# Two expert outputs per token: added in memory, or written side by side and added on chip

## The chip, the cores and the metric

The kernel runs on one core of a Trainium2 chip. The metric is the device time of one execution in microseconds (us). A core has a matrix engine (PE, with weight loads listed as PEld), a vector engine (DVE), a scalar engine (ACT), GpSimd (POOL) and a queue engine (SP) that issues most of the DMAs. GpSimd issues the DMAs whose rows are picked by a list of indices.

## The reference, cut to what matters

A transformer block runs first, then a hybrid layer on the same 1,024 tokens of width 1,024. The hybrid layer ends with a mixture of experts. Each token goes to two of 32 experts, so 2,048 token rows are spread over 32 lists, 64 rows to a list on average. Each expert is a gated pair of 1024x256 matrices and one 256x1024 matrix.

```python
def hierarchical_moe(h, ...):
    ...                                  # top group, then top-2 experts in it
    def expert_block(args):
        tok, wgt, e = args
        xb = h[tok]
        hid = jax.nn.silu(xb @ exp_gate[e]) * (xb @ exp_up[e])
        return (hid @ exp_down[e]) * wgt[:, None]
    ys = lax.map(expert_block, ...)
    return jnp.zeros((n, d), h.dtype).at[row_tok].add(ys.reshape(m_pad, d))

h = layer_norm_2(DEEPNORM_ALPHA * x + mixed, ln1_g, ln1_b)
ffn = hierarchical_moe(h.reshape(b * s, d), ...)
return layer_norm_2(DEEPNORM_ALPHA * h + ffn, ln2_g, ln2_b)
```

The output is the last norm of h plus the sum of the token's two expert rows. The kernel drops the common factor of h by scaling the weights and the epsilon.

## The kernel before, in words

All times and line numbers below are those of the profile. Until about 2,280 us the kernel runs the first block and the mixer. `output_mix` then makes h, 128 tokens at a time, and writes every piece to two scratch tensors in memory: `hd`, from which the experts read, and `acc`, to which they add (L1462). `route` builds, for each expert, a list of up to 128 token numbers and weights in `slots`; `tokens_of` turns it into integer row numbers `ids` (L1639). A place in a list that has no token points at one of 128 spare rows behind the last token.

`experts` runs a loop, written out in full, over 32 experts in a software pipeline. For expert e it gathers its 128 list places from `hd` (L1708; spare places are skipped by a bounds check), turns them with PE (L1719), splits rows and weights into a high and a low part (ACT L1695 and L1720, DVE L1696 and L1721), multiplies (L1731 to L1733), gates (L1738 to L1740), turns the hidden rows (L1747) and multiplies by the last matrix (L1762 to L1764). ACT scales the result into the tile `y` (L1765, two halves of 512 columns). There are three `y` buffers. Then GpSimd issues an indirect DMA that adds all 128 rows of `y` onto rows of `acc` (L1766):

```python
nc.gpsimd.indirect_dma_start(out=K.acc, out_offset=bass.IndirectOffsetOnAxis(ap=tok, axis=0), in_=y, in_offset=None,
                             compute_op=ALU.add)
```

The weights of an expert are three loads of 1 MiB from SP into a ring of ten `mraw` buffers (nine in one pool, one in another; L1663). In the texts here a *scatter* is the DMA of L1766, y(e) and scatter(e) are those of expert e, counted from 0.

After the loop SP loads the gain and bias of the last norm; `overflow` counts lists with more than 128 tokens and runs a loop over them whose number of turns is read from memory (none here). All engines pass that loop together. Behind it the last norm begins. SP loads eight tiles of `acc` (L1827, 128 tokens each, 0.5 MiB). Tiles 0, 2, 4 and 6 have their statistics made by DVE (L1842 to L1844), tiles 1, 3, 5 and 7 by ACT (L1836 to L1838) with a last multiply and bias by PE (L1856, L1857) and a copy by ACT (L1858). DVE multiplies by the gain in both (L1854, L1860) and finishes the even tiles (L1861). SP stores each tile (L1862).

The order on each engine is made at build time by a scheduler from the order of the program text. It puts a semaphore wait in front of an instruction that touches what an earlier one wrote; for a tensor in memory that is written through an index list it can't know which rows are meant.

Of the kernel before, what the change touches and what calls it, by code (L numbers as in the profile page):

```python
# [16 lines left out]
P = 128  # L17
# [1384 lines left out]
def output_mix(K, a, x2d, mixd, last, vs, aident, m, gains):  # L1402
# [5 lines left out]
    with ExitStack() as s:  # L1408
# [20 lines left out]
        for n_, tt in enumerate((4, 0, 1, 2, 3, 5, 6, 7)):  # L1429
            tsl = slice(tt * P, (tt + 1) * P)  # L1430
            v = vs[tt]
            at = slice(tt % 4 * P, (tt % 4 + 1) * P)
            mh, ml = (x[:, at] for x in last[tt // 4])
            stats = pool.tile([P, 2, 6], F, tag="lns", name=K.uid("lns"), bufs=2)
            if tt < KT // 2:
                src = v
                for c in range(2):
                    sl = slice(c * HB, (c + 1) * HB)
                    ps = pj.tile([P, HB], F, tag="pj", name=K.uid("pj"))
                    K.mm3(ps, mh, ml, wh[KT - 1][:, sl], wl[KT - 1][:, sl], True, True)  # L1440
                    nc.vector.tensor_tensor(v[c], ps, v[c], op=ALU.add)
                    nc.vector.bn_stats(stats[:, c], v[c])
            else:
                src = [None, None]

                def use(c, ps):
                    nc.vector.bn_stats(stats[:, c], ps)
                    src[c] = ps
                output_part(K, pj, "pj", x2d, mixd, aident, tt, v, use, [(mh, ml)])
            ex.ahead(n_)  # L1450
            mean, scale, shift = normalize(K, pool, stats, tt < KT // 2)
            for c in range(2):
                sl = slice(c * HB, (c + 1) * HB)
                if tt < KT // 2:
                    nc.scalar.activation(v[c], v[c], AF.Identity, bias=shift, scale=scale)
                    nc.vector.tensor_tensor(v[c], v[c], gain[c], op=ALU.mult)
                    nc.vector.tensor_tensor(v[c], v[c], bias[c], op=ALU.add)
                else:
                    nc.vector.scalar_tensor_tensor(v[c], src[c], mean, gain[c], op0=ALU.subtract, op1=ALU.mult)
                    nc.vector.scalar_tensor_tensor(v[c], v[c], scale, bias[c], op0=ALU.mult, op1=ALU.add)  # L1460
                for d in (K.hd, K.acc):
                    nc.sync.dma_start(d[tsl, sl], v[c])  # L1462
            pl = sm.tile([P, HB], F, tag="sm", name=K.uid("rl"))
            hts = []
            for g in range(2):
                pt = ht.tile([P, 4, P], F, tag="ht", name=K.uid("ht"))
                for q in range(4):
                    nc.tensor.transpose(pt[:, q], v[g][:, q * P:(q + 1) * P], K.ident)
                h_ = pool.tile([P, 4, P], F, tag=f"h{g}", name=K.uid("hT"), bufs=1)
                nc.scalar.activation(h_, pt, AF.Copy)  # L1470
                hts += [h_[:, q] for q in range(4)]
            for q in range(KT):
                nc.tensor.matmul(pl[:, :36], hts[q], wr[:, q], start=(q == 0), stop=(q == KT - 1))
            nc.vector.tensor_tensor(K.logits[:, tt], pl[:, :36], rb, op=ALU.add)
            if tt in (3, 5):
                places = route(K, pool, sm, *{3: (0, 4), 5: (4, 6)}[tt], "sm", dict(room=("room", 1), rows=("rows", 1), onehot=("onehot", 2)))
                places()
# [15 lines left out]
def routing_setup(K, pool):  # L1493
# [1 line left out]
    nc = K.nc  # L1495
    c = K.late
    K.hd = K.dram.tile([T + P, D], F, name="hd")
    K.acc = K.dram.tile([T + P, D], F, name="acc")
    K.logits = c.tile([P, KT, 36], F, name="logits")

    K.assign = c.tile([P, 4 + KT + 1, 32], R, name="assign")
# [10 lines left out]
    nc.gpsimd.iota(K.iota, pattern=[[1, P]], base=0, channel_multiplier=0, allow_small_or_imprecise_dtypes=True)  # L1512

    K.spare = c.tile([P, 1], F, name="spare")
    nc.gpsimd.iota(K.spare, pattern=[[0, 1]], base=T + 1, channel_multiplier=1, allow_small_or_imprecise_dtypes=True)
    K.slots = c.tile([P, 32, 2], F, name="slots")
    K.sent = c.tile([P, KT, 2, 3], F, name="sent")
    fill = pool.tile([P, HB], F, tag="NT", name="fill")
    nc.vector.memset(fill, 0.0)
    for c in range(2):  # L1520
        for d in (K.hd, K.acc):
            nc.sync.dma_start(d[T:T + P, c * HB:(c + 1) * HB], fill)


def route(K, pool, psum, t0, t1, tag, tags):
# [106 lines left out]
def tokens_of(K, pool, rows, n):  # L1632

    nc = K.nc
    m = pool.tile([P, n], F, name=K.uid("empty"))
    nc.vector.tensor_scalar(m, rows, 0.0, K.spare, op0=ALU.is_equal, op1=ALU.mult)
    nc.vector.scalar_tensor_tensor(m, rows, -1.0, m, op0=ALU.add, op1=ALU.add)
    ids = pool.tile([P, n], I32, name=K.uid("ids"))
    K.listed = nc.vector.tensor_copy(ids, m).ins  # L1639
    return ids  # L1640


class Experts:
# [29 lines left out]
def experts(K, a, ex, out):  # L1673
    nc, tc = K.nc, K.tc
    with ExitStack() as s:
# [75 lines left out]
            nc.vector.tensor_tensor(hl, pt[:, 0:2], hh.bitcast(F), op=ALU.subtract)  # L1751
            return hh, hl

        def down(hid, unit, tok, wgt):
            hh, hl = hid
            h, l = unit
            y = pool.tile([P, D], F, tag="y", name=K.uid("y"), bufs=3)
            for f in range(2):
                ps = yp.tile([P, HB], F, tag="y", name=K.uid("yps"))
                for q in range(2):  # L1760
                    sl = slice(q * D + f * HB, q * D + (f + 1) * HB)
                    nc.tensor.matmul(ps, hh[:, q], h[:, sl], start=q == 0, stop=False)  # L1762
                    nc.tensor.matmul(ps, hl[:, q], h[:, sl], start=False, stop=False)
                    nc.tensor.matmul(ps, hh[:, q], l[:, sl], start=False, stop=q == 1)  # L1764
                nc.scalar.activation(y[:, f * HB:(f + 1) * HB], ps, AF.Copy, scale=wgt)  # L1765
            nc.gpsimd.indirect_dma_start(out=K.acc, out_offset=bass.IndirectOffsetOnAxis(ap=tok, axis=0), in_=y, in_offset=None,  # L1766
                                         compute_op=ALU.add)

        def block(tok, wgt, eg, eu, ed):
            raws = [ex.load(w) for w in (eg, eu, ed)]  # L1770
            xg = gather(tok)
            units = [parts_of(raws, u) for u in range(3)]
            ps = gate_up(turned_rows(xg), units)
            down(turned_hidden(gated(ps)), units[2], tok, wgt)

        tok = lambda e: ids[:, e:e + 1]
        wgt = lambda e: K.slots[:, e, 1:2]
        raws = lambda e: [ex.raw[3 * e + i] for i in range(3)]
        NE = 32
        ex.ahead(ex.RAW + ex.MORE)  # L1780
        places = route(K, pool, tp, 6, KT, "tp", dict(room=("y", 3), rows=("sg", 2), onehot=("hh", 2)))
        ids = tokens_of(K, cst, K.slots[:, :, 0], 32)
        with tc.issue_after(K.listed):
            units = {0: [parts_of(raws(0), u) for u in range(3)]}
            places()
# [3 lines left out]
        for e in range(NE + 1):  # L1789
# [11 lines left out]
            if e < NE:  # L1801
                sg = gated(ps)
            if e > 0:
                down(hid.pop(e - 1), units.pop(e - 1)[2], tok(e - 1), wgt(e - 1))
            if n < NE:
                with tc.issue_after(K.listed) if e == 0 else nullcontext():
                    units[n].append(parts_of(raws(n), 1))
# [9 lines left out]
        g2, b2 = gains  # L1817

        nc.scalar.activation(pool.tile([P, 1], F, tag="sg", name="root"), K.ones[:, 0:1], AF.Sqrt)
        overflow(K, a, cst, tp, block, *ex.w)  # L1820

        v = [ex.pool.tile([P, 2048], F, tag="raw", name=K.uid("v"))[:, :D] for _ in range(KT - 1)]
        v.append(xgs[0])
        m = cst.tile([P, KT, 4], F, name="ln2m")
        stats = cst.tile([P, KT, 2, 6], F, name="ln2s")
        for tt in range(KT):
            nc.sync.dma_start(v[tt], K.acc[tt * P:(tt + 1) * P, :])  # L1827

        by_act = (1, 3, 5, 7)
        diag = [cst.tile([P, P], F, name=f"diag{i}") for i in range(2)]  # L1830
        for n0, n1 in ((0, 1), (1, 2), (2, 4), (4, 6), (6, 8)):
            for tt in range(n0, n1):
                if tt in by_act:
                    low = m[:, tt, 3:4]
                    junk = pool.tile([P, D], F, tag="y", name=K.uid("junk"), bufs=3)
# [3 lines left out]
                    nc.vector.tensor_scalar(m[:, tt, 2:3], m[:, tt, 1:2], 1.0 / D, EPS2, op0=ALU.mult, op1=ALU.add)  # L1839
                else:  # L1840
                    for c in range(2):
                        nc.vector.bn_stats(stats[:, tt, c], v[tt][:, c * HB:(c + 1) * HB])  # L1842
                    nc.vector.bn_aggr(m[:, tt, 0:2], stats[:, tt])
                    nc.vector.tensor_scalar(m[:, tt, 2:3], m[:, tt, 1:2], EPS2, None, op0=ALU.add)  # L1844
            r_ = sqrt_rsqrt(K, pool, m[:, n0:n1, 2], n1 - n0, f"lnr{n0}")
            for tt in range(n0, n1):
                scale = r_[:, tt - n0:tt - n0 + 1]
                mean, sign = (m[:, tt, 3:4], ALU.add) if tt in by_act else (m[:, tt, 0:1], ALU.subtract)
                if tt in by_act:
                    d = diag[tt // 2 % 2]  # L1850
                    nc.vector.tensor_scalar(d, K.ident, scale, None, op0=ALU.mult)  # L1851
                    for c in range(2):
                        sl = slice(c * HB, (c + 1) * HB)
                        nc.vector.scalar_tensor_tensor(v[tt][:, sl], v[tt][:, sl], mean, g2[:, sl], op0=sign, op1=ALU.mult)  # L1854
                        ps = yp.tile([P, HB], F, tag="y", name=K.uid("lnps"))
                        nc.tensor.matmul(ps, K.ident, b2[:, sl], start=True, stop=False)  # L1856
                        nc.tensor.matmul(ps, d, v[tt][:, sl], start=False, stop=True)  # L1857
                        nc.scalar.activation(v[tt][:, sl], ps, AF.Copy)  # L1858
                else:
                    nc.vector.scalar_tensor_tensor(v[tt], v[tt], mean, g2, op0=sign, op1=ALU.mult)  # L1860
                    nc.vector.scalar_tensor_tensor(v[tt], v[tt], scale, b2, op0=ALU.mult, op1=ALU.add)  # L1861
                nc.sync.dma_start(out[0, tt * P:(tt + 1) * P, :], v[tt])  # L1862

# [89 lines left out]
```

## Time and profile before

| what | us |
|---|---|
| median of 3 runs | 2773.17 (2771.62 to 2780.43) |
| the profiled execution, its own time | 2772.53 |
| its span, first to last instruction | 2770.8 |
| expert loop, from y(0) to y(31) | 2392.4 to 2715.4 |
| last norm, from its first load to the end | 2736.0 to 2770.8 |

Times in the rows are microseconds from the start of the span. A group such as `L1765 ACT ACTIVATE y<-yps,slots` is line, engine, operation, tile written and tiles read. What stands in brackets behind an instruction is how long its engine sat idle before it and what it waited for. Busy time of PE is modelled, so engines that show full aren't necessarily at their peak.

### The profile page before, as it was taken

How to read it: one execution, taken by the hardware profiler on the slowest of the kernel's cores; microseconds unless marked ns; L12 is line 12 of the kernel's file. 1: busy time of each engine (PE TensorE's matmuls, PEld its weight loads, DVE VectorE, ACT ScalarE, POOL GpSimd, SP SyncE). 2: the span in 40 equal slices, each digit the busy share in tenths (PEclk: the TensorE clock that was granted, in tenths of full speed). 3: DMA queues.
4: the chain of work that ended last, by engine and by line, in shares of the span. 5: the costliest groups of instructions: out<-in, count | busy, mean ns of one | idle time of the engine just before them, and what ended most of it. 6: DMA issues, size and time to landing. Idle time of an engine off the chain costs nothing. (4 is left out here: it accounts for less than half of the span.)

```text
span 2770.8 us, 41847 instructions
## 1 busy us (share of the span) xinstructions
PE 2575.8 (93%) x15826; PEld 1970.9 (71%) x15826; DVE 1765.3 (64%) x3760; ACT 1119.0 (40%) x1851; POOL 535.0 (19%) x505
## 2 busy tenths in 40 slices
PE   7899999998989999999999999999998998898884
PEld 4666677776767888888888777666666777686662
DVE  5667777778576333333334667677687557898884
ACT  5444555545353221222113332332233212687773
POOL 3224444443340000000000011111111100222220
PEclk9989999999999999999999999999998899899997
DMA  7312222223324111111113322322233354799985
GB/s 240 79 47 51 55 59 48 59 48 113 109 81 125 50 46 50 46 50 46 49 46 88 107 56 51 58 50 44 50 60 93 91 194 167 267 378 359 354 287 161
DMA packets 379281, 305.77 MB, mean 110 GB/s; under 512 B 170902, under 2 KB 326054, under 8 KB 366790
## 3 DMA queue, kind: packets, MB, share of 16 engines
q1 hardware_dynamic: 302070, 272.79, 30.8%
q0 software_dynamic: 76896, 30.25, 6.3%
q8 instruction: 125, 2.05, 0.3%
q14 instruction: 78, 0.64, 0.1%
q10 hardware_dynamic: 112, 0.04, 0.0%
HBM read 257.53 MB, written 52.90 MB: 112 GB/s over the span
## 5 line engine op out<-in xcount | busy, mean ns | idle before, releaser
L85 ACT ACTIVATE whi<-raw 128x512 fp32r<-128x512 f32 (+2 forms) x269 | 168.7, 627 | 649.3 <-PE pout L113 286.1
L87 DVE TENSOR_TENSOR wlo<-raw,whi 128x512 fp32r<-128x512 f32 (+2 forms) x269 | 194.4, 724 | 188.0 <-ACT whi L85 181.9
L112 PE MATMUL pj<-hi,whi 128*128 128x512 f32 x736 | 302.9, 412 | 1.9 <-ACT fz L412 1.9
L114 PE MATMUL pj<-hi,wlo 128*128 128x512 f32 x736 | 298.7, 406 | 0.8 <-DVE wlo L87 0.8
L113 PE MATMUL pj<-lo,whi 128*128 128x512 f32 x736 | 295.9, 402 | 0.0
L1696 DVE TENSOR_TENSOR mlo<-mraw,mhi 128x1024 fp32r<-128x1024 f32 x192 | 226.7, 1220 | 34.7 <-ACT mhi L1695 34.6
L796 DVE SCALAR_TENSOR_TENSOR x<-pout,mod,x 128x512 f32<-128x512 f32 x128 | 96.2, 752 | 196.1 <-PE pout L114 195.6
L114 PE MATMUL pout<-uh,wlo 128*128 128x512 f32 x512 | 204.8, 400 | 0.5 <-DVE wlo L87 0.5
L1695 ACT ACTIVATE mhi<-mraw 128x1024 fp32r<-128x1024 f32 x192 | 198.1, 1064 | 13.5 <-PE gu L1732 13.0
L113 PE MATMUL pout<-ul,whi 128*128 128x512 f32 x512 | 203.3, 397 | 0.0
L114 PE MATMUL pin<-hi,wlo 128*128 128x512 f32 x512 | 199.8, 390 | 2.5 <-DVE wlo L87 2.4
L112 PE MATMUL pout<-uh,whi 128*128 128x512 f32 x512 | 202.0, 394 | 0.0
L112 PE MATMUL pin<-hi,whi 128*128 128x512 f32 x512 | 199.6, 390 | 0.0
L113 PE MATMUL pin<-lo,whi 128*128 128x512 f32 x512 | 199.4, 389 | 0.0
L594 ACT ACTIVATE pe<-sps,nlo 128x512 f32<-128x512 f32 x192 | 110.3, 578 | 148.4 <-PE sps L592 57.7
L112 PEld LDWEIGHTS pj<-hi,whi 128*128 128x128 f32 x736 | 140.2, 191 | 36.7 <-issue 6.1
L599 POOL TENSOR_TENSOR pl<-pe,ph 128x512 fp32r<-128x512 f32 (+3 forms) x128 | 137.6, 1077 | 144.9 <-DVE ph L596 125.8
L114 PEld LDWEIGHTS pj<-hi,wlo 128*128 128x128 f32 x736 | 139.7, 190 | 33.9 <-issue 1.7
L113 PEld LDWEIGHTS pj<-lo,whi 128*128 128x128 f32 x736 | 140.2, 190 | 28.0 <-issue 2.1
L932 POOL DMA_DIRECT2D x2d<-x x8 | 4.4, 551 | 690.9 <-DVE x L796 687.8
L596 DVE CAST ph<-pe 128x512 fp32r<-128x512 f32 x192 | 94.9, 497 | 35.4 <-ACT pe L594 34.2
L1732 PE MATMUL gu<-mhi,xl 128*128 128x512 f32 x256 | 103.8, 406 | 14.2 <-DVE xl L1721 14.2
(613 smaller groups left out, 5918.3 us busy)
## 6 DMA issues: line engine op xcount, KB each, us to landing
mraw<-in_exp_gate SPq DMA_DIRECT2D x32, 1024.0 KB
mraw<-in_exp_up SPq DMA_DIRECT2D x32, 1024.0 KB
mraw<-in_exp_down SPq DMA_DIRECT2D x32, 1024.0 KB
raw<-in_w_mlp_in SPq DMA_DIRECT2D x72, 256.0 KB
adaw<-in_w_ada SPq DMA_DIRECT2D x64, 256.0 KB
raw<-in_w_mlp_out SPq DMA_DIRECT2D x64, 256.0 KB
raw<-in_fox_w_in SPq DMA_DIRECT2D x48, 256.0 KB
raw<-in_w_in SPq DMA_DIRECT2D x44, 256.0 KB
```

Of the source, the lines that this page charges most:

```text
L85: nc.scalar.activation(hi, raw, AF.Copy)
L87: nc.vector.tensor_tensor(lo, raw, hi.bitcast(F), op=ALU.subtract)
L112: mm(ps, wh, xh, start=start, stop=False)
L113: mm(ps, wh, xl, start=False, stop=False)
L114: mm(ps, wl, xh, start=False, stop=stop)
L594: nc.scalar.activation(pe[:, :wd], ps[:, :wd], AF.Exp, bias=nlo[:, st, hd:hd + 1])
L596: nc.vector.tensor_copy(ph[:, :wd], pe[:, :wd])
L599: eng.tensor_tensor(pl[:, :wd], pe[:, :wd], ph[:, :wd].bitcast(F), op=ALU.subtract)
L796: nc.vector.scalar_tensor_tensor(x[f][:, sl], ps, K.mod[:, 40 + f:41 + f], x[f][:, sl], op0=ALU.mult, op1=ALU.add)
L1695: nc.scalar.activation(view(h), src, AF.Copy)
L1696: nc.vector.tensor_tensor(view(l), src, view(h).bitcast(F), op=ALU.subtract)
L1732: nc.tensor.matmul(ps, xl[:, q], h[:, sl], start=False, stop=False)
```

## The change

The sum in memory goes. Memory gets a tensor `yd` with two rows for each token; the list now holds the row in `yd` (2 x token + 0 or 1), from which the token number is had by a shift. A scatter writes its rows without adding, and places without a token are skipped by a bounds check. `acc` and its writes go. After the expert loop, SP loads h itself (eight tiles, in front of `overflow`), and behind `overflow` eight tiles of `yd` of 1 MiB each, with both rows of a token side by side. The last norm adds three operands: DVE alone for tile 0, GpSimd (first with second row) and DVE (onto h) for tiles 1, 3, 5 and 7, and PE by three products with the identity for tiles 2, 4 and 6, whose sums stay in PSUM.

```diff
@@ output_mix
-                for d in (K.hd, K.acc):
-                    nc.sync.dma_start(d[tsl, sl], v[c])
+                nc.sync.dma_start(K.hd[tsl, sl], v[c])
@@ routing_setup
-    K.acc = K.dram.tile([T + P, D], F, name="acc")
+    K.yd = K.dram.tile([2 * T, D], F, name="yd")
-    nc.gpsimd.iota(K.spare, pattern=[[0, 1]], base=T + 1, ...)
+    nc.gpsimd.iota(K.spare, pattern=[[0, 1]], base=2 * T + 1, ...)
...
@@ route
-    nc.gpsimd.iota(sent[:, :, :, 0], pattern=[[P, G], [0, 2]], base=t0 * P + 1, channel_multiplier=1, ...)
+    nc.gpsimd.iota(sent[:, :, :, 0], pattern=[[2 * P, G], [1, 2]], base=2 * t0 * P + 1, channel_multiplier=2, ...)
@@ tokens_of
+    to = pool.tile([P, n], I32, name=K.uid("to"))
+    nc.vector.tensor_copy(to, m)
     ids = pool.tile([P, n], I32, name=K.uid("ids"))
-    K.listed = nc.vector.tensor_copy(ids, m).ins
-    return ids
+    K.listed = nc.vector.tensor_scalar(ids, to, 1, None, op0=ALU.arith_shift_right).ins
+    return ids, to
@@ experts, down
-            nc.gpsimd.indirect_dma_start(out=K.acc, out_offset=bass.IndirectOffsetOnAxis(ap=tok, axis=0), in_=y, in_offset=None,
-                                         compute_op=ALU.add)
+            nc.gpsimd.indirect_dma_start(out=K.yd, out_offset=bass.IndirectOffsetOnAxis(ap=to, axis=0), in_=y, in_offset=None,
+                                         bounds_check=2 * T - 1, oob_is_err=False)
@@ experts, the last norm
+        v = []
+        for i in range(KT // 2):
+            t = ex.pool.tile([P, 2048], F, tag="raw", name=K.uid("v"))
+            v += [t[:, :D], t[:, D:]]
+        for tt in range(KT):
+            nc.sync.dma_start(v[tt], K.hd[tt * P:(tt + 1) * P, :])
         overflow(K, a, cst, tp, block, *ex.w)
-        v = [ex.pool.tile([P, 2048], F, tag="raw", name=K.uid("v"))[:, :D] for _ in range(KT - 1)]
-        v.append(xgs[0])
+        room = [(ex.pool, "raw")] * 4 + [(ex.more, "raw"), (wp, "hi"), (wp, "lo"), (ex.pool, "raw")]
+        two = []
+        for tt, (from_, tag) in enumerate(room):
+            two.append(from_.tile([P, 2, D], F, tag=tag, name=K.uid("two")))
+            nc.sync.dma_start(two[tt], K.yd[2 * tt * P:2 * (tt + 1) * P].rearrange("(p k) f -> p k f", k=2))
...
-        for tt in range(KT):
-            nc.sync.dma_start(v[tt], K.acc[tt * P:(tt + 1) * P, :])
+        by_act, by_pe = (1, 3, 5, 7), (2, 4, 6)
...
+                ya, yb = two[tt][:, 0], two[tt][:, 1]
+                if tt in by_pe:
+                    src[tt] = [gu.tile([P, HB], F, tag="gu", name=K.uid("sum")) for _ in halves]
+                    for ps, sl in zip(src[tt], halves):
+                        for n, x in enumerate((v[tt], ya, yb)):
+                            nc.tensor.matmul(ps, K.ident, x[:, sl], start=n == 0, stop=n == 2)
+                else:
+                    src[tt] = [v[tt][:, sl] for sl in halves]
+                    (nc.gpsimd if tt in by_act else nc.vector).tensor_tensor(ya, ya, yb, op=ALU.add)
+                    nc.vector.tensor_tensor(v[tt], v[tt], ya, op=ALU.add)
...
-                        nc.vector.bn_stats(stats[:, tt, c], v[tt][:, c * HB:(c + 1) * HB])
+                        nc.vector.bn_stats(stats[:, tt, c], src[tt][c])
...
-                    nc.vector.scalar_tensor_tensor(v[tt], v[tt], mean, g2, op0=sign, op1=ALU.mult)
+                    for c, sl in enumerate(halves):
+                        nc.vector.scalar_tensor_tensor(v[tt][:, sl], src[tt][c], mean, g2[:, sl], op0=sign, op1=ALU.mult)
```

## Rows read from the trace of the kernel before

**Rows 1.** Loop's start: busy PE, PEld, DVE, ACT, POOL; clock, DMA share, GB/s.

```profile
2392.40:2467.00 74.60, 74.60 (x369) 62.85 (x368) 72.72 (x89) 68.60 (x98) 21.65 (x13) 1.00 1.00 361
```

**Rows 2.** Timeline of ACT: first halves of y(1), y(8), y(9), y(29); y(31).

```profile
2401.50 0.70 ACT L1765 ACTIVATE y<-yps,slots 128x512 f32<-128x512 f32 x1
...
2466.97 0.70 ACT L1765 ACTIVATE y<-yps,slots 128x512 f32<-128x512 f32 x1
...
2478.05 0.69 ACT L1765 ACTIVATE y<-yps,slots 128x512 f32<-128x512 f32 x1 [1.60 <-DMA acc<-y,ids]
...
2700.18 0.69 ACT L1765 ACTIVATE y<-yps,slots 128x512 f32<-128x512 f32 x1
...
2714.11 1.26 ACT L1765 ACTIVATE y<-yps,slots 128x512 f32<-128x512 f32 x2 [3.74 <-DMA acc<-y,ids]
```

**Rows 3.** Timeline of POOL: scatters 0, 7, 25, 30 and 31.

```profile
2393.94 2.57 POOL L1766 DMA_INDIRECT acc<-y,ids  x1 [2.23 <-ACT y L1765]
...
2478.73 1.71 POOL L1766 DMA_INDIRECT acc<-y,ids  x1 [8.19 <-ACT y L1765]
...
2682.20 1.58 POOL L1766 DMA_INDIRECT acc<-y,ids  x1 [8.27 <-ACT y L1765]
...
2721.60 1.54 POOL L1766 DMA_INDIRECT acc<-y,ids  x1 [5.31 <-DMA acc<-y,ids]
2728.48 1.54 POOL L1766 DMA_INDIRECT acc<-y,ids  x1 [5.34 <-issue]
```

**Rows 4.** DMAs of 2395 to 2470; of 2715 to 2735 and 2350 to 2362 (us to landing).

```profile
DMA packets 4957, 27.87 MB, mean 372 GB/s; under 512 B 1038, under 2 KB 1038, under 8 KB 2078
...
acc<-y,ids POOLq DMA_INDIRECT x3, 6.2
...
xg<-hd,ids POOLq DMA_INDIRECT x1, 4.5
```

**Rows 5.** The chain that ended last: SP's first load of the last norm.

```profile
2735.97 0.37 SPq L1827
```

**Rows 6.** Timeline of DVE and of PE in the last norm, first and last.

```profile
2739.59 1.29 DVE L1842 BATCH_NORM_STATS2 ln2s<-v 128x6 f32<-128x512 f32 x2 [26.56 <-DMA v<-acc]
...
2763.93 0.28 DVE L1851 TENSOR_SCALAR diag<-ident_r,rsq 128x128 f32<-128x128 f32 x1
...
2750.48 5.40 PE L1857 MATMUL lnps<-v,diag 128*128 128x512 f32 x6 [8.66 <-DVE diag L1851]
...
2760.01 1.88 PE L1857 MATMUL lnps<-v,diag 128*128 128x512 f32 x4
```

**Rows 7.** Groups of DVE in the last norm, and of the split in the loop.

```profile
L1860 DVE SCALAR_TENSOR_TENSOR v<-v,ln2m,ln_g 128x1024 f32<-128x1024 f32 x4 | 5.1, 1276 | 0.0
L1861 DVE SCALAR_TENSOR_TENSOR v<-v,rsq,ln_b 128x1024 f32<-128x1024 f32 x4 | 5.0, 1254 | 0.0
L1854 DVE SCALAR_TENSOR_TENSOR v<-v,ln2m,ln_g 128x512 f32<-128x512 f32 x6 | 4.4, 738 | 0.0
...
L1696 DVE TENSOR_TENSOR mlo<-mraw,mhi 128x1024 fp32r<-128x1024 f32 x167 | 197.0, 1220 | 28.6 <-ACT mhi L1695 28.6
```

**Rows 8.** Timeline: an addition on POOL beside one on DVE, then DVE's alone.

```profile
768.81 1.29 POOL L718 TENSOR_TENSOR sumsq<-sumsq,sq 128x512 f32<-128x512 f32 x1
769.29 1.37 DVE L87 TENSOR_TENSOR wlo<-raw,whi 128x512 fp32r<-128x512 f32 x1 [1.28 <-ACT whi L85]
771.24 0.68 DVE L87 TENSOR_TENSOR wlo<-raw,whi 128x512 fp32r<-128x512 f32 x1
```

**Rows 9.** Last norm, columns as in rows 1: during its loads; as PE's clock rises.

```profile
2742.00:2744.00 2.00, 0.00 (x0) 0.00 (x0) 0.85 (x4) 1.94 (x5) 0.00 (x0) 1.00 1.02 418
...
2754.00:2756.00 2.00, 2.00 (x4) 0.96 (x4) 2.00 (x5) 1.21 (x5) 0.00 (x0) 0.66 0.62 244
```

**Rows 10.** Waits of 2275 to 2366 for a DMA; making the index list.

```profile
ACT whi L85 <- DMA ozr<-x2d: 3.2, 1, 3.2
...
2360.55 0.18 DVE L1639 CAST ids<-empty 128x32 int32<-128x32 f32 x1
```

More of the change, by code (lines that the diff above doesn't have):

```diff
@@ L1514, in routing_setup @@
     K.spare = c.tile([P, 1], F, name="spare")
-    nc.gpsimd.iota(K.spare, pattern=[[0, 1]], base=T + 1, channel_multiplier=1, allow_small_or_imprecise_dtypes=True)
+    nc.gpsimd.iota(K.spare, pattern=[[0, 1]], base=2 * T + 1, channel_multiplier=1, allow_small_or_imprecise_dtypes=True)
     K.slots = c.tile([P, 32, 2], F, name="slots")
@@ L1520, in routing_setup @@
     for c in range(2):
-        for d in (K.hd, K.acc):
-            nc.sync.dma_start(d[T:T + P, c * HB:(c + 1) * HB], fill)
+        nc.sync.dma_start(K.hd[T:T + P, c * HB:(c + 1) * HB], fill)
 def route(K, pool, psum, t0, t1, tag, tags):
@@ L1586, in route @@
     nc.vector.tensor_tensor(w2, w1, ex, op=ALU.mult)
-    nc.gpsimd.iota(sent[:, :, :, 0], pattern=[[P, G], [0, 2]], base=t0 * P + 1, channel_multiplier=1, allow_small_or_imprecise_dtypes=True)
+    nc.gpsimd.iota(sent[:, :, :, 0], pattern=[[2 * P, G], [1, 2]], base=2 * t0 * P + 1, channel_multiplier=2, allow_small_or_imprecise_dtypes=True)
     A = []
@@ L1752, in turned_hidden, with down @@
             return hh, hl
-        def down(hid, unit, tok, wgt):
+        def down(hid, unit, to, wgt):
             hh, hl = hid
@@ L1765, in down, with block @@
                 nc.scalar.activation(y[:, f * HB:(f + 1) * HB], ps, AF.Copy, scale=wgt)
-            nc.gpsimd.indirect_dma_start(out=K.acc, out_offset=bass.IndirectOffsetOnAxis(ap=tok, axis=0), in_=y, in_offset=None,
-                                         compute_op=ALU.add)
-        def block(tok, wgt, eg, eu, ed):
+            nc.gpsimd.indirect_dma_start(out=K.yd, out_offset=bass.IndirectOffsetOnAxis(ap=to, axis=0), in_=y, in_offset=None,
+                                         bounds_check=2 * T - 1, oob_is_err=False)
+        def block(lists, wgt, eg, eu, ed):
+            tok, to = lists
             raws = [ex.load(w) for w in (eg, eu, ed)]
@@ L1773, in block @@
             ps = gate_up(turned_rows(xg), units)
-            down(turned_hidden(gated(ps)), units[2], tok, wgt)
+            down(turned_hidden(gated(ps)), units[2], to, wgt)
         tok = lambda e: ids[:, e:e + 1]
+        to = lambda e: rows[:, e:e + 1]
         wgt = lambda e: K.slots[:, e, 1:2]
@@ L1781, in experts @@
         places = route(K, pool, tp, 6, KT, "tp", dict(room=("y", 3), rows=("sg", 2), onehot=("hh", 2)))
-        ids = tokens_of(K, cst, K.slots[:, :, 0], 32)
+        ids, rows = tokens_of(K, cst, K.slots[:, :, 0], 32)
         with tc.issue_after(K.listed):
@@ L1803, in experts @@
             if e > 0:
-                down(hid.pop(e - 1), units.pop(e - 1)[2], tok(e - 1), wgt(e - 1))
+                down(hid.pop(e - 1), units.pop(e - 1)[2], to(e - 1), wgt(e - 1))
             if n < NE:
@@ L1819, in experts @@
         nc.scalar.activation(pool.tile([P, 1], F, tag="sg", name="root"), K.ones[:, 0:1], AF.Sqrt)
-        overflow(K, a, cst, tp, block, *ex.w)
-        v = [ex.pool.tile([P, 2048], F, tag="raw", name=K.uid("v"))[:, :D] for _ in range(KT - 1)]
-        v.append(xgs[0])
+        v = []
[4 more added lines that the diff above has]
+            nc.sync.dma_start(v[tt], K.hd[tt * P:(tt + 1) * P, :])
+        overflow(K, a, cst, tp, block, *ex.w)
+        room = [(ex.pool, "raw")] * 4 + [(ex.more, "raw"), (wp, "hi"), (wp, "lo"), (ex.pool, "raw")]
[3 more added lines that the diff above has]
+            nc.sync.dma_start(two[tt], K.yd[2 * tt * P:2 * (tt + 1) * P].rearrange("(p k) f -> p k f", k=2))
         m = cst.tile([P, KT, 4], F, name="ln2m")
         stats = cst.tile([P, KT, 2, 6], F, name="ln2s")
-        for tt in range(KT):
-            nc.sync.dma_start(v[tt], K.acc[tt * P:(tt + 1) * P, :])
-        by_act = (1, 3, 5, 7)
+        by_act, by_pe = (1, 3, 5, 7), (2, 4, 6)
         diag = [cst.tile([P, P], F, name=f"diag{i}") for i in range(2)]
+        halves = [slice(c * HB, (c + 1) * HB) for c in range(2)]
         for n0, n1 in ((0, 1), (1, 2), (2, 4), (4, 6), (6, 8)):
+            src = {}
             for tt in range(n0, n1):
+                ya, yb = two[tt][:, 0], two[tt][:, 1]
[8 more added lines that the diff above has]
+                    nc.vector.tensor_tensor(v[tt], v[tt], ya, op=ALU.add)
                 if tt in by_act:
@@ L1851, in experts @@
                     nc.vector.tensor_scalar(d, K.ident, scale, None, op0=ALU.mult)
-                    for c in range(2):
-                        sl = slice(c * HB, (c + 1) * HB)
+                    for c, sl in enumerate(halves):
                         nc.vector.scalar_tensor_tensor(v[tt][:, sl], v[tt][:, sl], mean, g2[:, sl], op0=sign, op1=ALU.mult)
@@ L1859, in experts @@
                 else:
-                    nc.vector.scalar_tensor_tensor(v[tt], v[tt], mean, g2, op0=sign, op1=ALU.mult)
+                    for c, sl in enumerate(halves):
+                        nc.vector.scalar_tensor_tensor(v[tt][:, sl], src[tt][c], mean, g2[:, sl], op0=sign, op1=ALU.mult)
                     nc.vector.scalar_tensor_tensor(v[tt], v[tt], scale, b2, op0=ALU.mult, op1=ALU.add)
```

## The prediction

> **What bounds the kernel now.** The chain that ended last is short: it holds only the last 50 us, the end of the expert loop and the last norm. It starts in the scatters of L1766, so I read the loop next, by stage. In its first 75 us PE is busy all the time and DVE 97% of it, at the granted clock 1.00 (2.4 GHz), with the DMA engines at a share of 1.00 [rows 1]. I then followed one instruction per expert, ACT's first half of `y`, along the timeline [rows 2]. From y(1) to y(8) it comes every (2466.97 - 2401.50) / 7 = 9.353 us. That is the pace of the compute engines. At y(9) ACT first sits idle, and it waits for a scatter. From there to y(29) the pace is (2700.18 - 2466.97) / 21 = 11.10 us.
>
> The scatters explain the change of pace [rows 3]. They are never in flight together: scatters 0 to 7 are issued every 12.11 us, 7 to 25 every 11.30 us, and the last two, when no weights are being loaded, 6.88 us apart, against 6.2 us from issue to landing [rows 4]. So each waits for the one before to land. y(e) needs the buffer that scatter(e - 3) reads. The chain of scatters is slower than compute from the start, and when the ring of three is used up, at y(9), it sets the pace. At the end it is three scatters behind: y(31) is done at 2715.37 [rows 2], scatter 31 is issued at 2728.48 and lands at 2734.7 [rows 3, 4]. All engines wait for it, and SP issues the last norm's loads at 2735.97 [rows 5]. From there to the first work of DVE it is 3.62 us, then DVE works with hardly a gap until 2764.21 (24.6 us), and PE, ACT and the last store take the remaining 6.6 us [rows 6].
>
> **The loop: -36.8 us.** At the free pace y(29) would come at 2401.50 + 28 x 9.353 = 2663.4 instead of 2700.18 [rows 2]. The new scatter must allow that. Unlike an addition, it need not read its destination, and on average 64 of its 128 rows are moved, the others skipped. I expect the scatters still to wait for each other, since the rows are picked at run time and the rows of before show that order. So the question is the period p of the chain. y(29) needs scatter(26) landed, about 0.8 us before the next can be issued: 2393.94 + 27p - 0.8 = 2663.4 gives p = 10.0. Up to that the loop loses nothing; each 0.1 us above costs 2.7 us. No row shows a plain scatter. Its upper bound is the old period, 12.1 in the loop's first part. The nearest row for a lower one is a gather, which also moves only rows with a token and skips the rest: 4.5 us to landing without other traffic, against 6.2 of the scatter [rows 4]. In proportion p = 12.1 x 4.5 / 6.2 = 8.8; with the same 1.7 us taken off, 10.4. I take 9.6 to 10.0, since part of the delay in the loop is waiting behind weights that stay, and so nothing lost.
>
> **The end of the loop: -9.5 us.** From y(29) to the landing of scatter 31 it was 34.5 us. With p = 9.9, scatter 27 is issued at 2661.2. The weights are then in, and the four that are left come at about 7 us once and 6.88 - 1.7 = 5.2 us three times: scatter 31 at 2683.8, landed 4.5 us later, 25.0 us behind y(29). Without any chain, y(31) would end 15.2 us behind y(29) and the landing follow 4.5 us later, 6 us better still. The upper bound is no gain.
>
> **The last norm: +16.3 us.** Four terms. (1) The first load is 1 MiB and not 0.5 MiB: at 418 GB/s [rows 9] that is +1.3. (2) DVE does six additions of 128x1024 more, two for tile 0 and one for each of tiles 1, 3, 5 and 7. At 1.22 us, the time of L1696 on the same shape [rows 7], that is +7.3. (3) The gain multiply of the even tiles is cut in two: 2 x 0.738 against 1.276, four times [rows 7], +0.8. Its reading from PSUM I take as free. (4) GpSimd makes four additions of 128x1024. By the 1.29 us of 128x512 one takes about 2.6 us. This isn't hidden, though GpSimd is idle: beside such an addition, DVE's subtraction of two operands took 1.37 us instead of 0.68 [rows 8]. It began when 0.81 us of the GpSimd instruction were left, and was late by 0.69. So DVE stands still while GpSimd adds, when its own instruction reads two operands from SBUF. Such instructions (L1854, L1860, L1861) make up about 16 of DVE's 24.6 us [rows 7], two thirds, so 4 x 2.6 x 2/3 = +6.9, between 0 and 10.4. The Trainium skill says it more strictly ("SBUF — State Buffer", SBUF: two separate sides): GpSimd and a DVE instruction with two SBUF inputs lock each other out for a whole instruction. By that rule taken in full the term would be 10.4 and the sum 3.5 us higher; by the row, 6.9.
>
> What this does not wait for: eight loads of 1 MiB take 20.2 us at 418 GB/s, so the last tile is there some 24 us after the first issue, while DVE ends at 3.6 + 1.3 + 24.6 + 15.0 = 44.5. PE has 18 products more, of two records each. At 2.4 GHz four records took 1.88 us [rows 6], so 17 us, beside 15 of the 16 products it had; together 32 us in 44. The loads of h, 4.2 MB or 10 us of transfer, are issued when the last experts' weight buffers come free, some 20 us before y(31), and lie under the end of the loop; uncovered they would cost up to 10 us.
>
> **The rest: +0.2 us.** `tokens_of` gets one more conversion of 128x32 on DVE, 0.18 us [rows 10], and all engines wait for the list there. The writes of `acc` by `output_mix` go, 16 DMAs of SP. PE waited for no DMA in that stretch; the only such wait is 3.2 us of ACT [rows 10]. I take 0, with up to -3.2.
>
> **Sum.** -36.8 - 9.5 + 16.3 + 0.2 = -29.8. Against the profiled execution's 2772.53 that is 2742.7; the median of the runs is 0.6 higher, so I forecast **2743**.
>
> **Rivals.** (A) *The chain keeps its pace.* If the delay of a scatter in the loop is mostly waiting behind weights, p stays 11.3. The loop then gains 36.8 - 27 x 1.3 = 1.7, the end some 8 (five scatters, 1.7 us less each), the last norm costs 16.3: 2779, slower than before. This decides from p = 11.05. For it: 11.3 is far above the 6.88 without weights. Against: the scatter's bytes halve. (B) *The chain goes.* If nothing makes a plain scatter wait for the last, only y(31) and one landing remain: 2737. The Trainium skill ("DMA: Bandwidth & Descriptors", Rules for kernel authors) asks for a wait on the earlier DMA's semaphore beside an accumulating DMA; the old order agrees, and two plain writes to different rows need none. (C) *The weights become the bound.* At 9.353 us an expert needs 3.15 MB of weights and 0.26 MB each of gather and scatter, 392 GB/s; the free stretch moved 372 [rows 4]. At that rate an expert takes 9.87 us, 28 of them +14: 2757. Against: the last norm's loads reach 418 [rows 9]. (D) *PE holds the last norm.* After an idle spell PE runs at 1.2 GHz: six records took 5.40 us [rows 6], and some 5 us later the granted clock is on its way up, 0.66 [rows 9]. Two such spells, with a sum that DVE waits for, add 9 us: 2752.
>
> **How the numbers follow.** The forecast 0.48, A 0.10, B 0.18, C 0.12, D 0.12. The forecast's own spread: no standstill of DVE beside GpSimd takes it to 2736, p = 10.4 and the skill's full lock to 2757. B with no standstill and ACT's 3.2 us gives 2727; C with D gives 2766. Leaving out A and the far ends, the range is 2727 to 2766. About 0.3% (8.3 us) is what a measurement of this kernel can tell from no change. Faster by more: all but A and a double mishap, 0.87; within, 0.05; slower, 0.08.
>
> **What would show it.** Right: `y` every 9.4 us up to the last expert, no ACT wait for a scatter; scatters still one at a time, 9 to 10 us apart; the last norm some 51 us from its first load; DVE's additions and multiplies stretched to over 2 us beside GpSimd's. Wrong: ACT waiting for scatters from about y(10) again (A); two scatters in flight (B); the split L1695 waiting for weights (C); DVE's statistics waiting for PE's sums (D). The forecast fails most easily in p, which no row of before gives, and in how the scheduler orders the last norm.

## The result, and the profile after

| | before | changed |
|---|---|---|
| median of the runs, us | 2772.88 (4 runs, 2771.62 to 2780.43) | 2745.02 (4 runs, 2739.69 to 2747.93) |
| profiled execution: time, span, us | 2772.53, 2770.8 | 2739.69, 2738.0 |

The changed kernel is faster by 27.9 us, a ratio of 0.9892 (95% interval 0.9868 to 0.9916). The forecast was 2743, with a range of 2727 to 2766. The two traces, cut where the prediction's terms meet:

| stage | before | after | difference | forecast |
|---|---|---|---|---|
| start to y(1) | 2401.5 | 2396.4 | -5.2 | +0.2 |
| y(1) to y(29) | 298.7 | 262.8 | -35.9 | -36.8 |
| y(29) to the last norm's first load | 35.8 | 22.9 | -12.9 | -9.5 |
| first load to the end | 34.8 | 55.9 | +21.1 | +16.3 |
| span | 2770.8 | 2738.0 | -32.8 | -29.8 |

The first row is not the change's: in the nine later profiles of kernels that share this stretch with the changed one, scatter 0 comes at 2392.9 to 2400.0, here at 2388.77. Without it the traces differ by 27.6 us, as the medians do.

ACT's first halves of y(1), y(8), y(9), y(29) and, last, the second half of y(31), on the timeline; they answer to [rows 2]:

```profile
2396.35 0.70 ACT L1766 ACTIVATE y<-yps,slots 128x512 f32<-128x512 f32 x1
...
2461.96 0.70 ACT L1766 ACTIVATE y<-yps,slots 128x512 f32<-128x512 f32 x1
...
2471.34 0.70 ACT L1766 ACTIVATE y<-yps,slots 128x512 f32<-128x512 f32 x1
...
2659.12 0.70 ACT L1766 ACTIVATE y<-yps,slots 128x512 f32<-128x512 f32 x1
...
2672.45 0.69 ACT L1766 ACTIVATE y<-yps,slots 128x512 f32<-128x512 f32 x1 [0.46 <-PE yps L1765]
```

The pace is 9.373 us before y(8) and 9.385 over all 28 experts; no row waits for a scatter. The loop's middle by windows, columns as in [rows 1], shows what is the bound now: PE without a gap, DVE 97.5%.

```profile
2461.00:2640.00 179.00, 179.00 (x879) 150.09 (x878) 174.53 (x212) 163.78 (x230) 47.29 (x38) 1.00 0.99 387
```

POOL's scatters 0, 7, 25 to 27, 30 and 31 on the timeline [rows 3]:

```profile
2388.77 1.97 POOL L1767 DMA_INDIRECT yd<-y,to  x1 [2.21 <-ACT y L1766]
...
2459.97 1.05 POOL L1767 DMA_INDIRECT yd<-y,to  x1 [6.83 <-ACT mhi L1696]
...
2631.80 1.80 POOL L1767 DMA_INDIRECT yd<-y,to  x1 [7.62 <-ACT y L1766]
2641.84 1.19 POOL L1767 DMA_INDIRECT yd<-y,to  x1 [6.77 <-DMA yd<-y,to]
2651.08 1.33 POOL L1767 DMA_INDIRECT yd<-y,to  x1 [8.05 <-ACT y L1766]
...
2671.91 0.96 POOL L1767 DMA_INDIRECT yd<-y,to  x1 [3.52 <-DMA yd<-y,to]
2676.22 0.96 POOL L1767 DMA_INDIRECT yd<-y,to  x1 [3.35 <-DMA ov_row<-ov_d]
```

The profile names an instruction of ACT for several of these waits, but y(25) was done at 2623.7 (its second half begins at 2622.96), 8 us ahead of its scatter: what is late is the scatter before. They still go one at a time, 9.55 us apart from 7 to 25 ((2631.80 - 2459.97) / 18), 9.72 from 0 to 27, and 4.3 for the last. Issue to landing takes 8.8 us in the loop's middle and 3.6 at its end, from the DMA views of 2470 to 2640 and of 2667 to 2682:

```profile
yd<-y,to POOLq DMA_INDIRECT x18, 8.8
...
yd<-y,to POOLq DMA_INDIRECT x3, 3.6
```

The trace has a landing for only 14 of these 18 scatters and for one of the three; in the control, the same kernel run once more (below), all have one, with 8.5 and 3.7. Before it was 6.2 at the end [rows 4], and in the same middle window:

```profile
acc<-y,ids POOLq DMA_INDIRECT x15, 10.3
```

The last norm, on the timelines of SP, POOL, DVE and PE [rows 5, 6]; in brackets what ended an idle time:

```profile
2682.06 4.14 SPq L1837 DMA_DIRECT2D two<-yd  x8
...
2689.43 2.34 POOL L1855 TENSOR_TENSOR two<-two 128x1024 f32<-128x1024 f32 x1 [12.25 <-DVE v L1856]
2694.41 2.35 POOL L1855 TENSOR_TENSOR two<-two 128x1024 f32<-128x1024 f32 x1 [2.64 <-DMA two<-yd]
2699.39 2.34 POOL L1855 TENSOR_TENSOR two<-two 128x1024 f32<-128x1024 f32 x1 [2.63 <-DMA two<-yd]
2705.04 2.35 POOL L1855 TENSOR_TENSOR two<-two 128x1024 f32<-128x1024 f32 x1 [3.31 <-DMA two<-yd]
...
2686.86 1.23 DVE L1855 TENSOR_TENSOR two<-two 128x1024 f32<-128x1024 f32 x1 [15.21 <-DMA two<-yd]
...
2691.02 1.30 DVE L1884 SCALAR_TENSOR_TENSOR v<-v,ln2m,ln_g 128x512 f32<-128x512 f32 x1
...
2694.55 3.30 DVE L1885 SCALAR_TENSOR_TENSOR v<-v,rsq,ln_b 128x1024 f32<-128x1024 f32 x1
...
2699.28 0.68 DVE L1866 BATCH_NORM_STATS2 ln2s<-sum 128x6 f32<-128x512 f32 x1
2699.89 1.85 DVE L823 TENSOR_TENSOR rsq<-rsq,ln2m 128x1 f32<-128x1 f32 x1
...
2705.67 2.93 DVE L1877 SCALAR_TENSOR_TENSOR v<-v,ln2m,ln_g 128x512 f32<-128x512 f32 x2
...
2715.76 0.70 DVE L1866 BATCH_NORM_STATS2 ln2s<-sum 128x6 f32<-128x512 f32 x1 [0.63 <-PE sum L1852]
...
2725.20 0.70 DVE L1866 BATCH_NORM_STATS2 ln2s<-sum 128x6 f32<-128x512 f32 x1 [3.13 <-PE sum L1852]
...
2729.41 0.28 DVE L1875 TENSOR_SCALAR diag<-ident_r,rsq 128x128 f32<-128x128 f32 x1
...
2703.80 3.78 PE L1880 MATMUL lnps<-v,diag 128*128 128x512 f32 x4 [8.20 <-DVE diag L1875]
...
2729.75 3.78 PE L1880 MATMUL lnps<-v,diag 128*128 128x512 f32 x4 [3.72 <-DVE diag L1875]
```

Beside each GpSimd addition one DVE row is stretched: 1.30 for some 0.74, 3.30 for 1.25, 1.85 for 0.15, 2.93 for 1.40, together about 5.8 us. DVE also waits twice for a sum of PE, 3.76 us. At the very end PE takes 3.78 us for four records (the trace's entries for its products), 1.88 in [rows 6]. The whole last norm by windows, columns as in [rows 1], has PE busy for 36.9 us at a mean granted clock of 0.77:

```profile
2682.00:2738.00 56.00, 36.93 (x68) 14.92 (x68) 38.07 (x70) 17.00 (x34) 9.37 (x4) 0.77 0.56 225
```

### The profile page after: what moved, and what is told of

It reads as the page before. It is cut to its first block, busy times and chain, and to the rows that moved or that the text cites. A ratio compares the mean times of both kernels' runs of the same rounds, so it can differ in the third digit from the quotient of the medians.

```text
span 2738.0 us, 41952 instructions
## 1 busy us (share of the span) xinstructions
PE 2576.5 (94%) x15862; PEld 1976.4 (72%) x15862; DVE 1778.4 (65%) x3771; ACT 1119.0 (41%) x1850; POOL 528.1 (19%) x509
## 5 line engine op out<-in xcount | busy, mean ns | idle before, releaser
L1696 ACT ACTIVATE mhi<-mraw 128x1024 fp32r<-128x1024 f32 x192 | 201.2, 1067 | 27.7 <-PE gu L1733 26.2
L113 PEld LDWEIGHTS pj<-lo,whi 128*128 128x128 f32 x736 | 140.4, 191 | 27.9 <-issue 2.1
L113 PEld LDWEIGHTS pout<-ul,whi 128*128 128x128 f32 x512 | 96.4, 188 | 24.6
```

Of the source, the lines that this page charges most:

```text
L113: mm(ps, wh, xl, start=False, stop=False)
L1696: nc.scalar.activation(view(h), src, AF.Copy)
```

## The experiments

Three numbers are read from each profile beside the median of the runs: the landing time of scatters in the loop's middle, the time from scatter 0's issue to scatter 31's, and the last norm from its first load to the end (for h_late from its first load of h). The ratios are to runs of the kernel before that were made beside each kernel, whose medians lie between 2769.6 and 2775.6. The trace of two_chains has no landings, and the 8.1 of odd_first_two_chains is of scatters of half the columns.

| kernel | median, us | ratio to before, 95% interval | landing | scatter 0 to 31 | last norm |
|---|---|---|---|---|---|
| before | 2772.88 | | 10.3 | 334.5 | 34.8 |
| changed | 2745.02 | 0.9892 (0.9868 to 0.9916) | 8.8 | 287.5 | 55.9 |
| add_skip | 2768.47 | 0.9984 (0.9963 to 1.0005) | 10.1 | 323.9 | 34.9 |
| all_rows | 2751.30 | 0.9909 (0.9880 to 0.9938) | 8.9 | 294.2 | 55.8 |
| add_into_yd | 2814.81 | 1.0163 (1.0142 to 1.0185) | 10.4 | 332.8 | 55.4 |
| ring_of_four | 2776.77 | 1.0010 (0.9993 to 1.0028) | 11.1 | 340.5 | 34.8 |
| two_chains | 2746.33 | 0.9894 (0.9877 to 0.9911) | | 285.5 | 59.7 |
| h_late | 2755.13 | 0.9920 (0.9891 to 0.9949) | 8.8 | 285.5 | 66.6 |
| adds_on_dve | 2743.24 | 0.9889 (0.9875 to 0.9903) | 8.7 | 287.2 | 53.8 |
| psum_room | 2739.45 | 0.9875 (0.9857 to 0.9893) | 8.4 | 287.5 | 49.9 |
| last_norm_edits | 2741.30 | 0.9882 (0.9867 to 0.9896) | 8.6 | 287.2 | 49.6 |
| control | 2744.56 | 0.9908 (0.9892 to 0.9925) | 8.5 | 287.4 | 55.3 |
| odd_first | 2739.05 | 0.9881 (0.9863 to 0.9899) | 8.6 | 289.1 | 48.4 |
| odd_first_two_chains | 2738.36 | 0.9883 (0.9864 to 0.9903) | 8.1 | 286.0 | 51.8 |

**What shortened the scatter.** Two things went at once: the addition, and the rows without a token. add_skip takes the second away from the kernel before, all_rows gives it back to the changed one.

```diff
-    in_=y, in_offset=None, compute_op=ALU.add)
+    in_=y, in_offset=None, bounds_check=T - 1, oob_is_err=False, compute_op=ALU.add)
```

> The kernel before, whose scatter still adds into `acc`, but skips the rows without a token. My theory: what shortens the scatter is mostly the half of the rows that it no longer moves. Then from issue to landing it comes down from 10.3 to 11.2 us towards the 8.8 of the changed kernel, the period falls below 10.0, and the loop and its end give back about 46 us while the last norm stays as it was: about 2727. Rival: it is the addition, the reading of the destination, that made the scatter slow. Then the scatters stay 11 us apart and the time stays at 2773. Both alike: the period falls to about 10.2 to 10.6, and the time lies between 2735 and 2755.

```diff
-    in_=y, in_offset=None, bounds_check=2 * T - 1, oob_is_err=False)
+    in_=y, in_offset=None)
...
-    K.yd = K.dram.tile([2 * T, D], F, name="yd")
+    K.yd = K.dram.tile([2 * T + P, D], F, name="yd")
```

> The changed kernel without the skipping: all 128 rows are written, the empty ones to 128 spare rows of `yd`. My theory (rows moved decide): issue to landing goes back to 10 us and more, ACT waits for scatters again from about y(10), and the loop and its end lose most of 46 us: 2775 to 2790. Rival (the addition decides): the scatters stay 9.4 us apart as compute gives them: 2745, no change.

My theory fell in both. With the addition and half the rows a scatter still takes 10.1 us, with all rows and no addition 8.9; the DMA views of 2470 to 2640, add_skip's and all_rows':

```profile
acc<-y,ids POOLq DMA_INDIRECT x16, 10.1
```

```profile
yd<-y,to POOLq DMA_INDIRECT x18, 8.9
```

The loop itself, from y(1) to y(29), takes 262.7 us in all_rows and 262.8 in the changed kernel, but 288.3 in add_skip (298.7 before): without the addition no skipping is needed. Of the chain from scatter 0 to 31, skipping is worth 10.6 us with the addition and 6.7 without. These are differences of one trace each; the changed kernel and the six others that have its loop and one chain spread from 285.5 to 289.1, and add_skip's profiled execution (2762.48) was 6 us faster than the median of its runs, whose ratio can't be told from no change. add_into_yd puts the addition alone back into the changed kernel; 32 writes of zeros ahead of the experts are more work than the changed kernel has.

```diff
-    in_=y, in_offset=None, bounds_check=2 * T - 1, oob_is_err=False)
+    in_=y, in_offset=None, bounds_check=2 * T - 1, oob_is_err=False, compute_op=ALU.add)
...
+    for i in range(2 * T // P):
+        nc.sync.dma_start(K.yd[i * P:(i + 1) * P, c * HB:(c + 1) * HB], fill)
```

> The changed kernel with one thing put back: the scatter adds to the rows of `yd`, which are set to zero ahead of the experts (32 writes of 256 KB more). Rows, skipping, loads and the last norm are the changed kernel's. My theory after the runs with skipping alone and with all rows: the addition sets the delay. A scatter then takes 10 to 11 us to land in the loop and about 6 us without other traffic, the period is 10.9 to 11.1, ACT waits for scatters again, and scatter 31 is issued some 324 us after scatter 0 as in the kernel with skipping alone (changed kernel: 287): 2745 + 37 + 1, some 2783, slower than before. Rival: without an addition a scatter of half the rows is fast enough whatever else it does, so with it the delay is only the 1 to 2 us longer that it is without traffic; the loop keeps 9.4 us and only the end loses 5 to 10 us: 2750 to 2755.

Landing is back at 10.4 us and ACT waits for scatters 22 times. Its scatter 0 comes only at 2417.36, 24 us after the control's, and the delay arises far ahead of any scatter: at 1500 us this kernel is 1 us behind the control, SP issues the writes of zeros from 1589.5 to 1612.2, and at 1740 us it is 27 behind. That is most of the 32 us by which it missed the expected 2783. From scatter 0 to the end it takes 395.8 us, the control 347.7 (2740.6 - 2392.93). So the addition alone is worth 48 us here, more than the whole gain. Its landing in the loop's middle, and its ACT line by what ended the waits:

```profile
yd<-y,to POOLq DMA_INDIRECT x15, 10.4
...
  DMA yd<-y,to: 55.6, 22
```

**What the chain holds up.** The kernel before with another `y` buffer:

```diff
-            y = pool.tile([P, D], F, tag="y", name=K.uid("y"), bufs=3)
+            y = pool.tile([P, D], F, tag="y", name=K.uid("y"), bufs=4)
```

> The kernel before with four `y` buffers in place of three. My theory: the chain of scatters sets the pace, the ring only says when it is felt. ACT's first wait comes some four or five experts later than y(9), but scatter 31 lands when it did: 2773, within 3 us. Rival: the ring is the bound, three buffers over a delay. With a fourth the experts go on at 9.35 us: 2773 - 36.8 = 2736.

The time stays, as the chain theory has it, but the reason that I gave for the pace was not whole. ACT waits for no scatter any more, and yet y(31) is done no sooner (2716.0; before 2715.4). The view of waits of 2480 to 2690 shows PE in its place, waiting for gathers, and POOL's timeline shows why: a gather stands in POOL's queue behind a scatter that waits for the one before.

```profile
PE xtp L1719 <- DMA xg<-hd,ids: 25.9, 16, 3.3
```

```profile
2581.10 2.05 POOL L1766 DMA_INDIRECT acc<-y,ids  x1 [8.41 <-ACT mhi L1695]
2583.46 1.42 POOL L1708 DMA_INDIRECT xg<-hd,ids  x1 [0.31 <-issue]
```

In two_chains `yd` is two tensors, one for each half of the columns:

```diff
-    K.yd = K.dram.tile([2 * T, D], F, name="yd")
+    K.yd = [K.dram.tile([2 * T, HB], F, name=f"yd{f}") for f in range(2)]
...
-            nc.gpsimd.indirect_dma_start(out=K.yd, ..., in_=y, ...)
+                nc.gpsimd.indirect_dma_start(out=K.yd[f], ..., in_=y[:, f * HB:(f + 1) * HB], ...)
```

> The changed kernel with `yd` split into two tensors by column halves, so that each expert has two scatters of 128x512, one to each. Theory: a scatter waits for the one before because both write one tensor. Then two scatters are in flight together, each chain of its own, and the last landing comes 1 to 3 us earlier, since y(31)'s first half need not wait for its second and the last scatters move half: 2743. Rival: GpSimd's queue takes one scatter at a time whatever it writes. Then the 64 scatters follow one another, each at half the bytes but nearly the whole delay, 8 us in the loop: the pace falls to some 14 us for an expert and the time goes over 2800.

Two scatters are in flight together: the last two are issued 1.39 us apart, right behind their halves of `y`. (No scatter of odd_first_two_chains, where the landings are recorded, landed in under 2.6 us.) So it is the common tensor that makes a scatter wait, not POOL's queue.

```profile
2679.63 0.97 POOL L1767 DMA_INDIRECT yd<-y,to  x1 [1.73 <-ACT y L1766]
2681.02 0.97 POOL L1767 DMA_INDIRECT yd<-y,to  x1 [0.42 <-issue]
```

From scatter 0 to the last norm's first load that is 1.4 us less (291.9 for 293.3), but only 0.5 less than the control's 292.4. The last norm takes 3.8 us more: its 16 half loads move 365 to 387 GB/s (windows of the changed kernel: 386 to 426), and DVE waits for sums for 2.66 and 2.65 us at the end. In all no gain.

**The last norm.** h_late moves the loads of h behind `overflow`:

> The changed kernel with the eight loads of h issued behind the overflow's loads, just ahead of those of `yd`, and no longer under the end of the loop. If they were hidden there, as I had it, they now cost their transfer, 4.2 MB or 10 us at 418 GB/s, ahead of the first addition: 2755. Rival: DVE and PE hold the last norm so firmly that they catch up with loads that come later: 2745 to 2748.

It costs 10.7 us of the last norm (66.6 against 55.9), 10.1 in the medians: the loads had been hidden. They were not quite free where they stood: scatters 27 to 31 take 21.9 us without them beside, 25.1 in the changed kernel and 24.9 to 27.7 in the five others that have this loop and one chain. From scatter 0 to the end h_late takes 356.6 us, the changed kernel 349.2 and the control 347.7.

adds_on_dve and psum_room change one line each:

```diff
-    (nc.gpsimd if tt in by_act else nc.vector).tensor_tensor(ya, ya, yb, op=ALU.add)
+    nc.vector.tensor_tensor(ya, ya, yb, op=ALU.add)
```

> The changed kernel with GpSimd's four additions of the last norm done by DVE. In the changed kernel's trace four DVE instructions beside them were stretched, by 0.6, 2.0, 1.7 and 1.5 us, 5.8 in all. My theory: DVE stands still when an instruction with two operands in SBUF meets a GpSimd addition, so 5.8 us go and 4 x 1.22 = 4.9 us come: the last norm (55.9 us from its first load) gets 1 us shorter, 2744, and no DVE addition or multiply takes longer than 1.3 us. Rival: the stretching has to do with waiting data and not with GpSimd. Then it stays and the additions are paid on top: 2750.

No DVE addition or multiply takes over 1.3 us any more for 128x1024, and the last norm is 2.1 us shorter (1 expected). The medians can't tell 1.8 us from nothing. The row that took 3.30 us is now:

```profile
2702.72 1.28 DVE L1885 SCALAR_TENSOR_TENSOR v<-v,rsq,ln_b 128x1024 f32<-128x1024 f32 x1
```

```diff
-    src[tt] = [gu.tile([P, HB], F, tag="gu", name=K.uid("sum")) for _ in halves]
+    from_, tag = (tp, "tp") if tt == 4 else (gu, "gu")
+    src[tt] = [from_.tile([P, HB], F, tag=tag, name=K.uid("sum")) for _ in halves]
```

> The changed kernel with tile 4's sums in the PSUM ring of the transposes, so that PE can make them while tile 2's still stand. In the changed kernel PE is idle for 8.2 us at 2695 and later makes DVE wait twice for a sum, 0.6 and 3.1 us. My theory: the two buffers for sums hold PE back, with a third and a fourth both waits go: 3.8 us shorter, 2741, the last norm 52 us. Rival: PE's clock or its order of work holds it; the waits stay: 2745.

The last norm is 6.0 us shorter in the trace; the median is 5.6 lower, with runs that overlap (2735.09 to 2746.51, and 2739.69 to 2747.93). DVE's waits for sums shrink from 3.76 to 0.60 us:

```profile
2718.73 0.70 DVE L1867 BATCH_NORM_STATS2 ln2s<-sum 128x6 f32<-128x512 f32 x1 [0.41 <-PE sum L1853]
...
2727.41 0.70 DVE L1867 BATCH_NORM_STATS2 ln2s<-sum 128x6 f32<-128x512 f32 x1 [0.19 <-PE sum L1853]
```

The end gains too: PE idles for 2.12 us ahead of its last four records instead of 3.72, and runs them at the granted clock 1.00 (2.4 GHz) instead of 0.50 (1.2 GHz), in 1.98 us instead of 3.78. The windows around those records, the changed kernel's and psum_room's, columns as in [rows 1]:

```profile
2729.70:2733.60 3.90, 3.78 (x4) 1.18 (x4) 0.00 (x0) 0.63 (x2) 0.00 (x0) 0.50 0.34 134
```

```profile
2733.00:2735.00 2.00, 1.97 (x4) 0.68 (x4) 0.00 (x0) 0.60 (x1) 0.00 (x0) 1.00 0.66 262
```

The next three put edits together, beside the changed kernel unaltered:

```diff
+                        if tt == 7 and c == 0:
+                            keep = tp.tile([P, HB], F, tag="tp", name="keep")
+                            for n in range(2):
+                                nc.tensor.matmul(keep, K.ident, m[:, 6, 2:3].to_broadcast([P, HB]), start=True, stop=True)
-            for tt in range(n0, n1):
-                scale = r_[:, tt - n0:tt - n0 + 1]
+            for tt in reversed(range(n0, n1)):
+                scale = r_[:, tt - n0:tt - n0 + 1]
```

> The changed kernel with four edits of the last norm: the additions on DVE (1.0 us), tile 4's sums in another PSUM ring (3.8 us), in each pair the odd tile's scaling ahead of the even one's, so that PE's and ACT's last work runs beside DVE's last multiply (1.3 us), and two products of nothing on PE ahead of the last ones, so that PE is at 2.4 GHz for them (3.78 to 1.88, 1.9 us). If they add up, 8 us: the last norm 48 us, 2737. Rival: DVE's work is the bound as soon as PE's waits are gone, and the last two edits only shift the wait to the store: 2741.

The last norm is 49.6 us, hardly less than with psum_room alone: the edits don't add up, since DVE now idles from 2726.9 to 2728.8 for ACT's statistics of tile 7.

> The four edits of the last norm, and in each pair the odd tile's sum and statistics ahead of the even one's too. In the four edits' trace DVE has no work from 2726.9 to 2728.8, because ACT's statistics of tile 7 start late. If that is the order's doing, the last norm goes from 49.6 to 47.7 us: 2737. Rival: what is moved ahead pushes the even tiles' statistics and the PE sums behind them, and DVE waits there instead: 49.6 or more, 2740.

> The kernel of odd_first with `yd` in two column halves. Two chains gave 2.0 us between the last `y` and the last norm's first load, and cost 3.8 us in the last norm, where eight loads of 1 MiB became sixteen of 0.5 MiB at 365 to 387 GB/s in place of 386 to 426. If it is the additions on GpSimd and the two PSUM buffers that made the slower loads felt, the last norm is now as long as in odd_first: 2735. If slower loads delay every tile, it gains nothing: 2739.

> The changed kernel once more, unaltered, beside the next three. If the 5 us by which its profiled execution reached scatter 0 early (2388.77 against 2393.94) belong to the change, scatter 0 comes at about 2389 again. If that stretch only varies from one execution to the next, as the seven profiles of the other kernels suggest (2391.9 to 2400.0), it comes anywhere in that range. The time: 2745 either way, within 4 us.

odd_first reverses the first loop over a pair as well. The last norm comes to 48.4 us, 1.2 of the 1.9 expected, though its chain took 1.7 us more than the control's. Its runs (2734.07 to 2740.35) lie wholly below the control's, made beside them (2741.4 to 2749.37): 5.5 us faster by the medians, and faster than both kernels. A second chain on top gains 2.2 us up to the first load, costs 3.4 in the last norm, and makes no difference that the medians show. The control reached scatter 0 at 2392.93, so the early 5 us were that one execution's.

## Why the prediction was right, point by point

**The loop.** Right in size: -35.9 for -36.8. The condition was a chain period up to 10.0; I took 9.9, and scatters 0 to 27 came every 9.72 us. It held by 0.28 us a scatter, or 7.6 us over the 27. The chain is still slower than compute (9.385), so the scatters fall behind and only the ring keeps this from being felt. Of the two reasons for a shorter p, that nothing is read from the destination and that half the rows are skipped, the first did the work, and the weight that I gave to the second, in my theory and in the choice of the gather as the nearest row, was wrong. Of the 47.0 us between scatter 0 and 31 the addition makes 40 with all rows moved, and 36 (add_skip) or 45 (add_into_yd) with half of them; with all rows and no addition (all_rows) scatters 0 to 27 came every 9.87 us, still under 10.0. So that p came out between the 8.8 and 10.4 taken from the gather is in part luck. That y's ring alone passes the delay on was not whole either: with a longer ring the gathers do it.

**The end of the loop.** -12.9 for -9.5. Scatter 27 was issued 8.0 us ahead of y(29), where p = 9.9 gave 2.2. The next two then came 8.2 and 8.1 us on, where I took 7 and 5.2: the weights were in, but I had not counted the loads of h, which run there (without them, in h_late, the four intervals take 21.9 us for 25.1). Without other traffic scatters come every 4.3 to 4.5 us, I took 5.2, and land in 3.6, I took 4.5 from the gather. The 15.2 us for y(31) without any chain was read where ACT waited for a scatter [rows 2] and is 14.0 here; "6 us better still" is 5.3 by its own numbers. Neither enters the sum.

**The last norm.** +21.1 for +16.3. By terms: the first load +1.2 (1.3 forecast), six additions 7.3 (7.3), the standstill beside GpSimd 5.8 (6.9). What failed is the step that held PE to have room, 32 us of 44. Its 68 records are the ones that were counted (busy for 36.9 us, since some ran at the granted clock 0.50); but its two buffers for sums left it idle early (8.20 us at 2695) and late when needed: 3.8 us of DVE's waits, and 1.7 at the end with the clock down. That is rival D in small; psum_room takes 6.0 us back. Nor were additions stretched, as I had named for a sign: all stay at 1.2 us, and it is multiplies and one 128x1 product that met GpSimd's. The 1.3 that remain hold the multiply cut in two (0.8 forecast).

**The rest.** The loads of h hid 10 us of the last norm, as priced, and slowed the last scatters. Removing the writes of `acc` gave nothing that ten profiles show: scatter 0 comes at 2388.8 to 2400.0 in them, and at 2391.9 to 2394.7 in the three that keep `acc`.

**The sum.** It is nearer than its terms: 3.4 us more were gained at the end of the loop, 0.9 less in the loop, and the last norm cost 4.8 more. That these nearly cancel is luck.

**The rivals.** A is out: p stayed well below 11.05; add_into_yd shows the loop that it meant. B: scatters still wait, by their common tensor, and two chains gain 0.5 to 1.4 us up to the first load. C: the loop moves 387 GB/s with PE never idle, and the weights hold nothing.

## What to carry to other kernels

When operations that wait for one another run slightly slower than compute, work out the period from which they stop mattering: here 10.0 us, and 1.5 us less of landing time was worth 36 us. An accumulating scatter cost that much more than a plain one, and dropping rows did little beside it. What such a change moves into a last stage should be laid out by buffers and order, not by sums of busy time.

## What was not expected of the hardware

A scatter that adds takes 6.1 us to land at the least (before), with half its rows skipped 5.9 (add_skip), and a plain one of all rows 3.3 (all_rows). That this addition costs more than half of the transferred rows was not in my estimate.

A DVE instruction of 128x1 took 1.85 us beside GpSimd's addition (0.15 otherwise), and it reads two tiles in SBUF. The statistics of 0.68 us just ahead of it, with one input, in PSUM, were not held although the addition had begun, nor were those of tile 0 at 2689.38, with one input in SBUF:

```profile
2689.38 1.29 DVE L1866 BATCH_NORM_STATS2 ln2s<-v 128x6 f32<-128x512 f32 x2
```

The rule that I had weighed, in the Trainium skill ("SBUF — State Buffer", SBUF: two separate sides), that the two lock each other out for a whole instruction, agrees: each of the four stretched rows ends after GpSimd's addition, by its ordinary length less 0.1 to 0.2 us. Yet the four additions, 9.4 us, cost 5.8, since DVE had other work for part of the time.
